# A hybrid decoder block on one core: the second MLP matrix by seven products of halves, and new first and last steps

## The chip, the cores and the metric

The kernel runs on one core of a Trainium2 chip. The metric is the device time of one execution in microseconds (us). It was run three times beside the profiled execution. The engines are named as in the profile: PE is TensorE (PEld its weight loads), DVE is VectorE, ACT is ScalarE, POOL is GpSimd, and SP is the queue that issues most of the DMA transfers.

## The reference

One decoder layer on x of 512 tokens by 1024 channels, all in float32:

```python
u = rmsnorm(x, g_norm_mix)
x = x + mixer_block(u, ...)          # mLSTM, GLA and gated DeltaNet, merged by gates, then w_out
u = rmsnorm(x, g_norm_mlp)
x = x + jnp.square(jax.nn.relu(u @ w_mlp_in)) @ w_mlp_out   # 1024 -> 4096 -> 1024
return rmsnorm(x, g_final)
```

The mixer has three branches of 4 heads of 128 channels. The root-mean-square norms divide each token by the root of its mean square. The two MLP matrices have 1024 x 4096 and 4096 x 1024 elements.

## The kernel before, in words

**Precision.** A float32 matmul is made of three matmuls of a faster type (float32r). Each operand is split into a high part (a cast to float32r) and a low part (the operand less its high part, again float32r); `mm3` (L603) issues low x high, high x low and high x high into one PSUM tile. So each weight piece costs a DMA load (`load_w`, L677, pieces of 128x1024; `load_w1`, L688, pieces of 128x512), a cast ("either": the planner picks ACT or DVE) and a subtraction on DVE. Work that is not split (transposes, attention, token sums) is plain float32 on TensorE.

**The planner.** `write_block` records every operation in a graph (`Graph.record`, L156; the profile shows all of them at L525, the line that emits). `Graph.schedule` (L243) gives an order for each engine: the split matmuls, the "mains", go to TensorE in the order of the stages in `plan` (L536); all other operations get a latest start (`due`, L275) and a list scheduler (`run`, L321) fills the engines by cost estimates, with PSUM and SBUF tiles from pools. `EVAC` (L47) says how long after its matmuls a PSUM tile should have been read, and L468 assumes DMA at 190 GB/s. The emitted order is fixed; each engine works in order.

**Pools.** 44 slots "s" of 128x512; three buffers each of "raw", "wh" and "wl" (128x1024) for weight pieces and their parts; 8 PSUM banks, four "g" for split products and four "m" for the rest.

**The first steps.** `NWARM` (L24) = 10 float32 matmuls of ones come first on TensorE. The parameters `pr` and most of the constants `cs` are loaded through POOL's queue, the rest of `cs` through ACT's. Stage "mv" (L767 to L779) multiplies the unnormalised x, in 8 k-steps, with the mv weights into four token tiles: each k-step loads an x tile and a 128x512 weight piece, scales and splits x (vh, vl), splits the weights, and issues 4 token tiles x 3 matmuls, the three of a tile together. `gen_u` (L649) squares the channel-major x tiles, adds them up on DVE, and sums over channels with `token_sums` (L638), four float32 matmuls against a column of ones; from this comes rc, 1/rms of each token.

**The MLP.** `gen_x2` (L1361) does the same sums for the second norm while it transposes x2T (channel-major) into x2 (token-major, 4 token tiles by 2 halves of 512 channels). The MLP goes by 8 groups of 512 hidden channels. `mlp_in` (L1402) makes, for each of 4 pieces of 128 hidden channels, 8 k-steps x 3 matmuls, then relu on ACT, its square as high part (`ah`, ACT), the square again on DVE (`rl`) and the low part (`al`, DVE). `mlp_out` (L1420) multiplies a group's 512 hidden channels with 512x1024 weights: 2 halves x 4 token tiles x 4 k-steps x 3 matmuls, each tile then added into x2 by one DVE instruction with the factor r2c (1/mean square of the token). The stages alternate: mi1, mo0, mi2, mo1, and so on to mi7, mo6, mo7. In the last group the tiles go half by half, the last in two pieces of 256 columns; `square_of` (L1456) sums the squares, and `finish` (L1463) takes 1/rms by a sqrt, a reciprocal and a correction, scales and stores a token tile.

Of the kernel before, what the change touches and what calls it, by code (L numbers as in the profile page):

```python
# [14 lines left out]
P = 128  # L15
# [8 lines left out]
NWARM = 10  # L24
# [22 lines left out]
EVAC = 5.0  # L47
# [62 lines left out]
class Op:  # L110
    __slots__ = ("i", "eng", "calls", "cost", "lat", "preds", "succs", "tiles", "main", "fset", "kind", "start", "fin", "lst", "npred", "ready", "new", "tag", "nbytes", "evac", "alts")


class Graph:
    def __init__(self, nc):
# [6 lines left out]
        self.gate = []  # L122
# [17 lines left out]
    def after(self, view):  # L140

        self.gate = [o for o, w, *_ in view.t.acc if w]

# [12 lines left out]
    def record(self, eng, method, a, k):  # L156
# [18 lines left out]
        self.gate = []  # L175
# [99 lines left out]
    def due(self, pin, end):  # L275
# [45 lines left out]
    def run(self, mains, caps, horizon, verbose=False):  # L321
# [19 lines left out]
        for o in ops:  # L341
            o.npred = len(o.preds)
            if any(t.cls == "m" for t in o.new):
# [44 lines left out]
        while done < total:  # L388
# [78 lines left out]
            if o.kind == "dma":  # L467
                dma_free = max(dma_free, T + 0.5) + o.nbytes / 190e3  # L468
# [67 lines left out]
def plan():  # L536

    seq = """mv mo dk0 mq1 sc mk0 dq1 dq0 mk1 mq0 dk1 gt01 dv0 gt00 dv1 gt02 lq0 gt03 gt20 up00 up02 lk0 lq1 lv lk1 up03 dz up01
    gt22 gt13 up20 gt12 gt21 up21 lr gt23 up22 up23 gt10 up10 up12 gt11 up11 up13 wo mi0""".split()
    for g in range(1, 8):  # L540
        seq += [f"mi{g}", f"mo{g - 1}"]
# [9 lines left out]
def hybrid_block(ctx, tc, xT, w_cm, w_tm, w_sc, w_up, w_out, w_mi, w_mo, w_lr, prm, cst, g_fin, out):  # L551
    nc = Graph(tc.nc)
    write_block(nc, xT, w_cm, w_tm, w_sc, w_up, w_out, w_mi, w_mo, w_lr, prm, cst, g_fin, out)
# [10 lines left out]
def write_block(nc, xT, w_cm, w_tm, w_sc, w_up, w_out, w_mi, w_mo, w_lr, prm, cst, g_fin, out):  # L564
# [58 lines left out]
    nc.gpsimd.dma_start(pr, prm)  # L623
    nc.gpsimd.dma_start(cs[:, :C_LV], cst[:, :C_LV])
# [13 lines left out]
    def token_sums(pss, sums):  # L638
        for t in range(4):
            mm(pss[:, t:t + 1], sums[:, blk(t)], ones)  # L640

    pss = mps("pss")
    rc = one("rc", [P, 4])


    for i in range(NWARM):
        mm(pss[:, P:2 * P], onem, onem)

    def gen_u():  # L649
# [8 lines left out]
        nc.vector.tensor_scalar(v, pss[:, :4], 1.0 / D, EPS, op0=ALU.mult, op1=ALU.add)  # L658
# [29 lines left out]
    def load_w1(src, name):  # L688
# [4 lines left out]
        nc.either.copy(h_, r)  # L693
# [72 lines left out]
    pmv = [gps(f"mvp{t}") for t in range(4)]  # L766
    for k in range(8):  # L767
# [9 lines left out]
        wh, wl = load_w1(w_tm[G_MV, k // 2, :, k % 2], f"mv{k}")  # L777
        for t in range(4):
            mm3(pmv[t], h_[:, blk(t)], l_[:, blk(t)], wh, wl, k == 0, k == 7)  # L779
# [11 lines left out]
    nc.scalar.dma_start(cs[:, C_LV:], cst[:, C_LV:])  # L791
# [14 lines left out]
    eall = one("em", [P, 4, 4, 2, P])  # L806
# [527 lines left out]
    def lv_evac(t, ps):  # L1334
        lv[t] = slot(f"lv{t}")
# [22 lines left out]
    pss2 = mps("pss2")  # L1358
    r2c = one("r2c", [P, 4])

    def gen_x2():  # L1361
        acc = slot("x2acc")
        for d in range(8):
            sq = tmp(f"x2sq{d}") if d else acc
            nc.scalar.activation(sq, x2T[d], AF.Square)
            if d:
                nc.vector.tensor_add(acc, acc, sq)
            if d == 7:
                token_sums(pss2, acc)
            if d % 4 == 3:  # L1370
                hf = d // 4
                for t in range(4):
# [4 lines left out]
                    nc.either.copy(x2[t][hf], ps)  # L1377
        v = small("v4", 4)
        nc.vector.tensor_scalar(v, pss2[:, :4], 1.0 / D, EPS, op0=ALU.mult, op1=ALU.add)
        nc.vector.reciprocal(r2c, v)  # L1380

# [18 lines left out]
    gf = [None, None]  # L1400

    def mlp_in(g):  # L1402
        hs_ = []
        stage[0] = f"mi{g}"
        for i in range(4):
            wh, wl = load_w(w_mi[g * 4 + i], f"mi{g}{i}")
# [11 lines left out]
        return hs_  # L1418

    def mlp_out(g, hs_):  # L1420
        last = g == NG - 1
        stage[0] = f"mo{g}"
        wts = []
        for hf in range(2):
            w_ = []
            for i in range(2):
                if last and hf:
                    w_ += [load_w1(w_mo[g, hf, i, :, kk], f"mo{g}{hf}{i}{kk}") for kk in range(2)]
                else:
                    wh, wl = load_w(w_mo[g, hf, i], f"mo{g}{hf}{i}")  # L1430
                    w_ += [(wh[:, kk], wl[:, kk]) for kk in range(2)]
            wts.append(w_)
        if last:

            for hf, t, c0, n in [(hf, t, 0, 512) for hf in range(2) for t in range(3)] + [(0, 3, 0, 512), (1, 3, 0, 256), (1, 3, 256, 256)]:
# [134 lines left out]
```

## Time and profile before

| what | value |
|---|---|
| time, median of 3 runs | 976.89 us (976.88 to 976.90) |
| the profiled execution's own time | 976.91 us |
| its span, first to last instruction | 975.1 us |
| mean granted TensorE clock | 0.996 |
| PE, DVE, ACT busy | 964.2, 580.9, 408.5 us |
| instructions | 12773 |
| DMA | 94.64 MB, mean 97 GB/s |

A profile is one execution. Busy time is the share in which an engine works on an instruction; matmuls are pipelined, so a matmul is shown as 0.39 us long though one starts every 0.23 us, and a busy TensorE may still run at half clock. What an engine waited for stands in brackets behind the row of the instruction that waited. A clock of 1.00 is 2.4 GHz and 0.50 is 1.2 GHz.

### The profile page before, as it was taken

How to read it: one execution, taken by the hardware profiler on the slowest of the kernel's cores; microseconds unless marked ns; L12 is line 12 of the kernel's file. 1: busy time of each engine (PE TensorE's matmuls, PEld its weight loads, DVE VectorE, ACT ScalarE, POOL GpSimd, SP SyncE). 2: the span in 40 equal slices, each digit the busy share in tenths (PEclk: the TensorE clock that was granted, in tenths of full speed). 3: DMA queues.
4: the chain of work that ended last, by engine and by line, in shares of the span. 5: the costliest groups of instructions: out<-in, count | busy, mean ns of one | idle time of the engine just before them, and what ended most of it. 6: DMA issues, size and time to landing. Idle time of an engine off the chain costs nothing.

```text
span 975.1 us, 12773 instructions
## 1 busy us (share of the span) xinstructions
PE 964.2 (99%) x4992; PEld 804.0 (82%) x4992; DVE 580.9 (60%) x1065; ACT 408.5 (42%) x764; POOL 5.4 (1%) x20
## 2 busy tenths in 40 slices
PE   8999999999999999999999999999999999999996
PEld 7888888888888888888888888888888888888885
DVE  6667867778525765777647665444454445544446
ACT  6454466533523664544244434442423233232313
POOL 0000000000000000000000000000000000000000
PEclk9999999999999999999999999999999999999998
DMA  7222532222411222212224222222323224322302
GB/s 269 87 87 87 170 113 95 57 87 88 123 58 66 75 98 87 88 66 76 75 89 142 96 90 94 86 98 87 108 87 109 88 84 153 128 87 87 108 22 87
DMA packets 37028, 94.64 MB, mean 97 GB/s; under 512 B 7804, under 2 KB 11900, under 8 KB 36968
## 3 DMA queue, kind: packets, MB, share of 16 engines
q1 hardware_dynamic: 36152, 92.51, 29.5%
q10 hardware_dynamic: 720, 1.08, 0.3%
q8 instruction: 39, 0.64, 0.3%
q0 software_dynamic: 96, 0.24, 0.1%
q14 instruction: 21, 0.17, 0.1%
HBM read 91.17 MB, written 2.65 MB: 96 GB/s over the span
## 4 chain that ended last, share of the span: by engine, by line
PE 98%; DVE 0%; DMA 0%; ACT 0%; issue 0%; DVEq 0%; POOLq 0%
PE mop L525 20%; PE mip L525 18%; PE upp L525 7%; PE wop L525 4%; PE mvp L525 2%; PE lrp L525 2%; PE dzp L525 2%; PE lvp L525 2%; PE ll L525 2%; PE gt22p L525 1%; PE gt13p L525 1%; PE gt20p L525 1%; PE gt12p L525 1%; PE gt21p L525 1%; PE dq0p L525 1%; PE dv0p L525 1%
## 5 line engine op out<-in xcount | busy, mean ns | idle before, releaser
L525 DVE SCALAR_TENSOR_TENSOR x<-mop,r2c,x 128x512 f32<-128x512 f32 (+1 forms) x65 | 48.1, 741 | 54.0 <-PE mop L525 53.9
L525 DVE TENSOR_TENSOR lw<-lbs 128x260 f32<-128x260 f32 (+12 forms) x52 | 21.0, 448 | 7.9 <-PE ll L525 7.8
L525 DVE SCALAR_TENSOR_TENSOR sg<-sg,upp 128x512 f32<-128x512 f32 x24 | 16.4, 685 | 15.5 <-PE upp L525 15.4
L525 ACT ACTIVATE lw<-lw 128x512 f32<-128x512 f32 x28 | 17.4, 630 | 14.1 <-DVE lw L525 13.8
L525 DVE TENSOR_TENSOR al<-rl,ah 128x512 fp32r<-128x512 f32 x32 | 22.0, 689 | 0.8
L525 DVE TENSOR_TENSOR rl<-rl 128x512 f32<-128x512 f32 x32 | 22.1, 692 | 0.0
L525 PEld LDWEIGHTS ll<-lwq,lw 128*17 128x17 f32 (+3 forms) x320 | 17.5, 131 | 4.3 <-issue 1.4
L525 ACT ACTIVATE ah<-rl 128x512 fp32r<-128x512 f32 x32 | 20.3, 634 | 1.0
L525 ACT ACTIVATE rl<-mip 128x512 f32<-128x512 f32 x32 | 18.9, 591 | 0.0
L525 ACT ACT_TABLE_LOAD x14 | 18.0, 1283 | 1.4 <-PEq L1558 1.2
L525 PE MATMUL ll<-lwq,lw 128*17 128x16 f32 (+3 forms) x320 | 17.9, 214 | 0.0
L525 DVE TENSOR_TENSOR x2T<-xr,wop 128x512 f32<-128x512 f32 x8 | 5.5, 686 | 13.3 <-PE wop L525 13.3
L525 DVE TENSOR_TENSOR lw<-lw,lks 128x260 f32<-128x260 f32 (+6 forms) x28 | 13.1, 498 | 0.0
L525 ACT COPY lAT<-ll 17x64 f32<-17x64 f32 (+3 forms) x32 | 7.2, 231 | 11.4 <-PE ll L525 11.0
L525 DVE COPY_PREDICATED lAT<-cs,ll 128x256 f32<-128x256 uint8 x16 | 9.3, 578 | 4.0 <-PE ll L525 4.0
L525 ACT ACTIVATE fsq<-x 128x512 f32<-128x512 f32 (+1 forms) x9 | 5.3, 585 | 14.1 <-DVE x L525 14.1
L525 DVE TENSOR_TENSOR me<-me,mqk 128x512 f32<-128x512 f32 (+3 forms) x16 | 7.5, 485 | 6.2 <-PE mqk L525 5.9
L525 DVE TENSOR_TENSOR sg<-sg,sg 128x512 f32<-128x512 f32 x16 | 10.8, 688 | 0.2
L525 ACT ACTIVATE cvs<-cv 128x512 f32<-128x512 f32 x12 | 7.5, 628 | 7.4 <-DVE cv L525 7.4
L525 PEld LDWEIGHTS mn<-mv,me 128*128 128x128 f32 x80 | 10.1, 191 | 0.5
L525 ACT ACTIVATE yh<-sg 128x512 fp32r<-128x512 f32 x8 | 5.1, 632 | 13.0 <-DVE sg L525 13.0
L525 PE MATMUL mqk<-mqs,mks 128*128 128x512 f32 (+3 forms) x32 | 10.4, 432 | 0.0
(1584 smaller groups left out, 3178.5 us busy)
## 6 DMA issues: line engine op xcount, KB each, us to landing
xk<-in_xT_dram SPq DMA_DIRECT2D x8, 256.0 KB, 5.6
em<-scr_rows SPq DMA_DIRECT2D x16, 128.0 KB, 4.6
xr<-in_xT_dram SPq DMA_DIRECT2D x8, 256.0 KB, 5.1
nm<-scr_rows SPq DMA_DIRECT2D x4, 256.0 KB, 3.7
out_dram<-x ACTq DMA_DIRECT2D x4, 256.0 KB, 2.1
out_dram<-x SPq DMA_DIRECT2D x4, 256.0 KB, 2.4
mo00r<-in_w_tm_dram SPq DMA_DIRECT2D x1, 512.0 KB, 6.0
mo01r<-in_w_tm_dram SPq DMA_DIRECT2D x1, 512.0 KB
```

Source lines behind the costliest of these rows:

```text
L525: getattr(getattr(nc, eng), method)(*[f(x) for x in a], **{n: f(x) for n, x in k.items()})
```

## The change

1. In groups 0 to 6 the product of a 512x512 block of hidden activations, seen as 2x2 blocks of 256, with the 512x1024 weights (2x2 blocks of 256x512) is made by Winograd's form of Strassen's algorithm: 7 products of half-size blocks in place of 8, with 4 sums of activation blocks and 4 of weight blocks ahead of them (DVE, the weight sums in place in four fixed buffers `bq`, which lie in the tile `eall` of the mixer). Products 1 and 6 accumulate over the groups in four PSUM banks; 5 and 7 in SBUF; 2, 3 and 4 are added into x2. In group 6 the shared sums are joined into x2 (`join`), and products 2 and 3 stay in PSUM, where the last group's first tiles go on.
2. `mlp_in` leaves the squares whole, in blocks by token half; the split is made later, for each product's operand.
3. The last group keeps eight products' worth of work; its tiles go token by token, its weights come in 128x512 pieces; `finish` takes the sqrt with the sum of the other pieces as its bias and fuses the multiplication by g_final.
4. The norms' sums are made token-major: x is loaded again as `x_tm` and squared with an accumulator on ACT; x2 is squared as its transposes leave PSUM. `token_sums` is gone.
5. The first steps: 9 warm-up matmuls, into the last mv tile; `pr` through ACT's queue; all of `cs` by one later load on SP's queue; the first k-step in the order high x high for four tiles, low x high for four, high x low for four; its weight cast on DVE.
6. The planner: `EVAC` 1.0 and another rule for it, 330 GB/s for DMA, "follow" (an operation that is to start after another, with no wait emitted), and stages split so that mi pieces and products alternate. lv takes mv's tiles.

```diff
-NWARM = 10
+NWARM = 9
-EVAC = 5.0
+EVAC = 1.0
...
-                l = min([l] + [pin[p] + p.cost + EVAC for p in o.preds if p in pin])
+                l = min(l, max((pin[p] + p.cost for p in o.preds if p in pin), default=1e9) + EVAC)
...
-                dma_free = max(dma_free, T + 0.5) + o.nbytes / 190e3
+                dma_free = max(dma_free, T + 0.5) + o.nbytes / 330e3
...
     for g in range(1, 8):
-        seq += [f"mi{g}", f"mo{g - 1}"]
+        seq += [x if x[0] == "p" else f"mi{g}{x[1]}" for x in "c0 p1 p5 c1 p7 p6 c2 p3 p4 c3 p2".replace("p", f"p{g - 1}").split()]
...
-    nc.gpsimd.dma_start(pr, prm)
-    nc.gpsimd.dma_start(cs[:, :C_LV], cst[:, :C_LV])
+    nc.scalar.dma_start(pr, prm)
...
     def gen_u():
-        acc = slot("xacc")
-        for k in range(8):
-            sq = tmp(f"xsq{k}") if k else acc
-            nc.scalar.activation(sq, xk[k], AF.Square)
-            if k:
-                nc.vector.tensor_add(acc, acc, sq)
-        token_sums(pss, acc)
+        ss = small("ss", 4)
+        for t in range(4):
+            b = eall.rearrange("p h c a t -> p (h c a t)")[:, blk(t, D)]
+            nc.follow(vh[4 + t // 2])
+            nc.sync.dma_start(b, x_tm[t])
+            nc.scalar.activation(b, b, AF.Square, accum_out=ss[:, t:t + 1])
...
+        wh, wl = load_w1(w_tm[G_MV, k // 2, :, k % 2], f"mv{k}", "vector" if k == 0 else None)
+        if k == 0:
+            for i, (a, b) in enumerate(((h_, wh), (l_, wh), (h_, wl))):
+                for t in range(4):
+                    with nc.group(stage[0]):
+                        nc.tensor.matmul(pmv[t], a[:, blk(t)], b, start=i == 0, stop=False)
+            continue
+        if k == 5:
+            nc.follow(x_)
+            nc.sync.dma_start(cs, cst)
...
-            a_h = slot("ah", F32R)
-            a_l = slot("al", F32R)
-            nc.scalar.activation(a_h, rl, AF.Square)
-            nc.vector.tensor_mul(rl, rl, rl)
-            nc.vector.tensor_sub(a_l, rl, a_h.bitcast(F32))
-            hs_.append((a_h, a_l))
+            for th in range(2):
+                nc.scalar.activation(a[i // 2][th][:, blk(i % 2, 256)], rl[:, blk(th, 256)], AF.Square)
...
+    def split_b(x, nm):
+        h_ = nc.tile("wh", [P, 2, 512], F32R, nm + "h")
+        l_ = nc.tile("wl", [P, 2, 512], F32R, nm + "l")
+        nc.either.copy(h_, x)
+        nc.vector.tensor_sub(l_, x, h_.bitcast(F32))
+        return h_, l_
...
+        (a11, a21), (a12, a22) = a
+        b11, b12, b21, b22 = bq
+        for x, hf, i in ((b11, 0, 0), (b12, 1, 0), (b22, 1, 1), (b21, 0, 1)):
+            nc.sync.dma_start(x, w_mo[g, hf, i])
+        tail = g == NG - 2
+        def product(n, x, y, nm):
+            stage[0] = f"p{g}{n}"
+            xh_, xl_ = split_a(x, f"a{nm}")
+            yh_, yl_ = split_b(y, f"b{g}{nm}")
+            out_ = []
+            bank = {1: p1, 6: p6, **({2: p1, 3: p6} if tail else {})}.get(n)
+            for t in range(2):
+                ps = bank[t] if bank else gps(f"pp{g}{n}{t}")
+                keepon = bank is not None
+                for k in range(2):
+                    c = slice(k * 256 + t * P, k * 256 + t * P + P)
+                    mm3(ps, xh_[:, c], xl_[:, c], yh_[:, k], yl_[:, k], k == 0 and (g == 0 or n not in (1, 6)), k == 1 and (tail and n in (1, 6) or not keepon))
+                out_.append(ps)
+            return out_
+        product(1, a11, b11, "11")
...
+        s1 = slot("S1")
+        nc.vector.tensor_add(s1, a21, a22)
+        nc.vector.tensor_sub(b11, b12, b11)
+        for t, ps in enumerate(product(5, s1, b11, "S1")):
...
+                nc.vector.tensor_add(p5[t], p5[t], ps)
+        s2 = slot("S2")
+        nc.vector.tensor_sub(s2, s1, a11)
+        nc.vector.tensor_sub(a21, a11, a21)
+        nc.vector.tensor_sub(b12, b22, b12)
+        for t, ps in enumerate(product(7, a21, b12, "S3")):
...
+        nc.vector.tensor_sub(b11, b22, b11)
+        product(6, s2, b11, "S2")
+        if tail:
+            join()
+        s4 = slot("S4")
+        nc.vector.tensor_sub(s4, a12, s2)
+        for t, ps in enumerate(product(3, s4, b22, "S4")):
...
+        nc.vector.tensor_sub(b11, b11, b21)
+        for t, ps in enumerate(product(4, a22, b11, "22")):
...
+        for t, ps in enumerate(product(2, a12, b21, "12")):
...
+        for t in range(2):
+            v = slot(f"v{t}")
+            nc.vector.tensor_add(v, us[t], p6[t])
+            add(t, 0, us[t])
+            nc.vector.tensor_add(us[t], v, p5[t])
+            add(t, 1, us[t])
+            nc.vector.tensor_add(p7[t], p7[t], v)
+            add(2 + t, 0, p7[t])
+            nc.vector.tensor_add(p5[t], p5[t], p7[t])
+            add(2 + t, 1, p5[t])
...
-        nc.scalar.activation(s, v, AF.Sqrt)
+        l = f[:, nsq[t] - 1:nsq[t]]
+        nc.scalar.activation(s, l, AF.Sqrt, bias=e)
+        nc.vector.tensor_add(v, l, e)
         nc.vector.reciprocal(y, s)
...
+        nc.vector.tensor_scalar(s, y, v, s, op0=ALU.mult, op1=ALU.add)
+        nc.vector.reciprocal(y, s)
...
+        a, b = x2[t]
+        nc.vector.scalar_tensor_tensor(b[:, 256:], b[:, 256:], y, gf[1][:, 256:], op0=ALU.mult, op1=ALU.mult)
+        nc.vector.tensor_scalar_mul(b[:, :256], b[:, :256], y)
+        nc.sync.dma_start(out[blk(t), blk(1, 512)], b)
+        nc.scalar.mul(a, a, y)
+        nc.scalar.dma_start(out[blk(t), blk(0, 512)], a)
```

## Rows read from the trace of the kernel before

**Rows 1.** The page: busy time of the engines, and the chain that ended last.
```profile
PE 964.2 (99%) x4992; PEld 804.0 (82%) x4992; DVE 580.9 (60%) x1065; ACT 408.5 (42%) x764; POOL 5.4 (1%) x20
...
PE 98%; DVE 0%; DMA 0%; ACT 0%; issue 0%; DVEq 0%; POOLq 0%
```

**Rows 2.** Stretch 700 to 960: length, busy of each engine, clock, DMA share, GB/s.
```profile
700.00:960.00 260.00, 260.00 (x1149) 215.29 (x1148) 126.83 (x156) 79.04 (x104) 0.00 (x0) 1.00 0.28 91
```

**Rows 3.** Groups by shape, DVE and ACT: busy us, mean ns of one, idle before.
```profile
L525 DVE SCALAR_TENSOR_TENSOR x<-mop,r2c,x 128x512 f32<-128x512 f32 x61 | 45.7, 749 | 52.7 <-PE mop L525 52.7
L525 DVE TENSOR_TENSOR rl<-rl 128x512 f32<-128x512 f32 x32 | 22.1, 692 | 0.0
...
L525 DVE TENSOR_TENSOR mi11l<-mi11r,mi11h 128x1024 fp32r<-128x1024 f32 x1 | 1.2, 1226 | 2.9 <-ACT mi11h L525 2.9
...
L525 DVE TENSOR_SCALAR lgw<-lge 128x512 f32<-128x512 f32 x4 | 1.7, 421 | 0.1
...
L525 ACT ACTIVATE ah<-rl 128x512 fp32r<-128x512 f32 x32 | 20.3, 634 | 1.0
L525 ACT ACTIVATE rl<-mip 128x512 f32<-128x512 f32 x32 | 18.9, 591 | 0.0
...
L525 ACT CAST mi10h<-mi10r 128x1024 fp32r<-128x1024 f32 x1 | 1.1, 1055 | 3.2 <-PE mip L525 3.2
```

**Rows 4.** Timeline of DVE in the MLP: start, length, instruction, idle before.
```profile
695.98 1.22 DVE L525 TENSOR_TENSOR mo100l<-mo100r,mo100h 128x1024 fp32r<-128x1024 f32 x1 [2.87 <-ACT mo100h L525]
697.13 0.69 DVE L525 TENSOR_TENSOR rl<-rl 128x512 f32<-128x512 f32 x1
```

**Rows 5.** Timeline of PE around the second norm's token sums.
```profile
622.39 0.95 PE L525 MATMUL pss<-ones,x2acc 128*128 128x1 f32 x8
...
623.20 0.48 PE L525 MATMUL mip<-uh,mi00l 128*128 128x512 f32 x1
...
623.52 0.39 PE L525 MATMUL mip<-ul,mi00h 128*128 128x512 f32 x1
```

**Rows 6.** Stretch 8 to 9 us, columns as in rows 2.
```profile
8.00:9.00 1.00, 1.00 (x4) 0.76 (x3) 1.00 (x2) 1.00 (x3) 0.00 (x0) 0.50 1.04 399
```

**Rows 7.** Timeline of the start, ACT and PE.
```profile
0.73 0.41 ACTq L525 DMA_DIRECT2D cs<-in_cst_dram  x1
...
1.05 3.98 PE L525 MATMUL pss<-onem 128*128 128x128 f32 x20 [1.05 <-DVE onem L525]
...
4.65 0.20 ACT L525 ACTIVATE scl<-pr 128x1 f32<-128x1 f32 x1 [2.19 <-DMA pr<-in_prm_dram]
4.76 0.70 ACT L525 ACTIVATE vh<-xk,pr 128x512 fp32r<-128x512 f32 x1
...
5.37 0.61 ACT L525 ACTIVATE xacc<-xk 128x512 f32<-128x512 f32 x1
...
5.89 0.60 ACT L525 CAST mv0h<-mv0r 128x512 fp32r<-128x512 f32 x1
...
6.54 0.51 PE L525 MATMUL mvp<-mv0h,vl 128*128 128x512 f32 x1 [1.51 <-ACT mv0h L525]
...
7.27 0.55 PE L525 MATMUL mvp<-mv0l,vh 128*128 128x512 f32 x1 [0.22 <-DVE ones L525]
...
14.24 0.39 PE L525 MATMUL mvp<-mv2h,vl 128*128 128x512 f32 x1
```

**Rows 8.** DMA issues of the start: KB each, us from issue to landing.
```profile
cs<-in_cst_dram ACTq DMA_DIRECT2D x1, 32.0 KB, 3.0
```

**Rows 9.** Timeline of the tail.
```profile
966.72 0.28 PE L525 MATMUL mop<-mo7111h,ah 128*128 128x256 f32 x1
...
968.35 0.20 ACT L525 ACTIVATE fs<-fv 128x1 f32<-128x1 f32 x1 [0.28 <-DVE fv L525]
...
968.83 0.15 DVE L525 RECIPROCAL fy<-fs 128x1 f32<-128x1 f32 x1
...
970.05 1.45 DVE L525 TENSOR_SCALAR x<-x,fy,fh 128x512 f32<-128x512 f32 x3
```

More of the change, by code (lines that the diff above doesn't have):

```diff
@@ L110 @@
 class Op:
-    __slots__ = ("i", "eng", "calls", "cost", "lat", "preds", "succs", "tiles", "main", "fset", "kind", "start", "fin", "lst", "npred", "ready", "new", "tag", "nbytes", "evac", "alts")
+    __slots__ = ("i", "eng", "calls", "cost", "lat", "preds", "succs", "tiles", "main", "fset", "kind", "start", "fin", "lst", "npred", "ready", "new", "tag", "nbytes", "evac", "alts", "soft")
 class Graph:
@@ L142, in after, with follow @@
         self.gate = [o for o, w, *_ in view.t.acc if w]
+    def follow(self, view):
+        self.soft = [o for o, w, *_ in view.t.acc if w]
     def group(self, key):
@@ L342, in run @@
             o.npred = len(o.preds)
+            for p in o.soft:
+                if p not in o.preds:
+                    waiting.setdefault(p, []).append(o)
+                    o.npred += 1
             if any(t.cls == "m" for t in o.new):
@@ L636, in write_block, with gen_u @@
     nc.vector.memset(onem, 1.0)
-    def token_sums(pss, sums):
-        for t in range(4):
[L640 to L649, printed above, removed]
-        acc = slot("xacc")
-        for k in range(8):
-            sq = tmp(f"xsq{k}") if k else acc
-            nc.scalar.activation(sq, xk[k], AF.Square)
-            if k:
-                nc.vector.tensor_add(acc, acc, sq)
-        token_sums(pss, acc)
+    eall = one("em", [P, 4, 4, 2, P])
+    rc = one("rc", [P, 4])
+    pmv = [gps(f"mvp{t}") for t in range(4)]
+    for i in range(NWARM):
+        with nc.group("warm"):
+            mm(pmv[3][:, :P], onem, onem)
+    def gen_u():
+        ss = small("ss", 4)
+        for t in range(4):
+            b = eall.rearrange("p h c a t -> p (h c a t)")[:, blk(t, D)]
+            nc.follow(vh[4 + t // 2])
+            nc.sync.dma_start(b, x_tm[t])
+            nc.scalar.activation(b, b, AF.Square, accum_out=ss[:, t:t + 1])
         v = small("v4", 4)
-        nc.vector.tensor_scalar(v, pss[:, :4], 1.0 / D, EPS, op0=ALU.mult, op1=ALU.add)
+        nc.vector.tensor_scalar(v, ss, 1.0 / D, EPS, op0=ALU.mult, op1=ALU.add)
         rsqrt(rc, v, 4)
@@ L1400, in write_block @@
     gf = [None, None]
+    bw = eall.rearrange("p h c a t -> p (h c a t)")
+    bq = [bw[:, blk(i, 1024)].rearrange("p (k n) -> p k n", k=2) for i in range(4)]
+    p1, p6 = [mps(f"P1{t}") for t in range(2)], [mps(f"P6{t}") for t in range(2)]
+    p5, p7, us = [None, None], [None, None], [None, None]
     def mlp_in(g):
-        hs_ = []
-        stage[0] = f"mi{g}"
+        a = [[slot(f"A{kh}{th}") for th in range(2)] for kh in range(2)]
         for i in range(4):
+            stage[0] = f"mi{g}{i}"
             wh, wl = load_w(w_mi[g * 4 + i], f"mi{g}{i}")
@@ new lines, in join, with add @@
+    def join():
+        def add(t, hf, v):
+            nc.vector.scalar_tensor_tensor(x2[t][hf], v, r2c[:, t:t + 1], x2[t][hf], op0=ALU.mult, op1=ALU.add)
+        for t in range(2):
+            v = slot(f"v{t}")
[7 more added lines that the diff above has]
+            add(2 + t, 1, p5[t])
@@ L1422, in mlp_out, with mlp_last @@
+    def mlp_last(a):
+        g = NG - 1
         stage[0] = f"mo{g}"
+        hs_ = [split_a(a[kh][th], f"z{kh}{th}") for kh in range(2) for th in range(2)]
         wts = []
@@ L1446, in mlp_out @@
[L1446 to L1451 removed]
+                w_ += [load_w1(w_mo[g, hf, i, :, kk], f"mo{g}{hf}{i}{kk}") for kk in range(2)]
+            wts.append(w_)
```

145 lines of the change are left out of this document (76 added, 69 removed).

## The prediction

> **What bounds the kernel now.** I read the page's totals first, then the chain that ended last, then the stretches, then the group durations. TensorE is busy 99% of the span and makes 98% of the chain [rows 1]: it is the bound, and an edit pays only if it shortens TensorE's own stream or the idle ends. The stretch from 700 to 960 us holds nothing but the MLP: 1149 matmuls in 260.00 us, 0.2263 us each, at granted clock 1.00, with VectorE busy 126.83 us (49%) and ScalarE 79.04 us (30%) [rows 2]. So there is no wait to remove there, but there is cover on the two other engines. At both ends TensorE does stand: at the start it works at half rate and waits; at the end 8 us follow its last matmul.
>
> **The sum is made** against the profiled execution's 976.91 us (span 975.1 and 1.8 around it); the runs' median is 976.89, the same to 0.02. About 0.2% (2 us) is what a measurement of this kernel can tell from no change.
>
> **1. Seven products for eight, groups 0 to 6.** Before, a group has 8 output tiles of 4 k-steps by 3 matmuls: 96. After, 7 products of 2 tiles, 2 k-steps, 3 matmuls: 84, of the same 128x512 shape. Twelve fewer in 7 groups is 84, by 0.2263 us [rows 2]: **-19.0 us**, all on the bounding engine. Group 7 keeps 96.
>
> The price is paid by VectorE. Before, a group has 8 weight subtractions of 1.226, 4 each of rl and al at 0.69 and 8 evictions of 0.749 [rows 3]: 21.3 us of a group's 192 matmuls, 43.5 us; 49%, as measured. After: 4 subtractions for the first matrix 4.9; 7 splits of an activation half (0.69) and a weight half (1.226) 13.4; 4 sums of activation halves 2.8; 4 of weight halves 4.9; 10 evictions 7.5 (products 1 and 6 stay in PSUM). That is 33.5 us in 180 matmuls, 40.7 us: 82%. Back to back the 1.22 us subtraction is followed after 1.15 us [rows 4], so nearer 76%. ScalarE: 11 casts of 1.055, 7 of about 0.63 (ah's row), 4 relu of 0.591, 8 squares of 256 columns (none is shown so far from the tail; bounds 0.32, half of ah, and 0.634; I take 0.42): 21.8 us, 54%. Neither becomes the bound on its own. The cover is thin in the last such group: joining the sums adds 16 operations (11.5) less 4 evictions (3.0), group 7's one-piece weight loads add 8 subtractions (5.5), its activation splits 4 (2.8): 50.3 us against 40.7. Some of the joining may slide into group 7's 21.7 us of matmuls, where I count 15 us of VectorE's own work; 65 us into 62.4, 95% at the back-to-back pace. What is late next is the first matmul of group 7 or the last tile. I take **+1.5 us** of waits in all; ends 0 (all covered) and 8 (a wait of about 1 us in each group and one at the join).
>
> DMA bytes of the MLP are unchanged. The weight halves now land in four fixed buffers, so their issue on SP's queue waits for the last reader, and the loads of the first matrix queue behind it; a buffer is released some 16 us (product 4's 2.7, then 5.4, 2.7 and 5.4 of matmuls) before its new content is due, against a DMA share of 0.28 [rows 2]. Nothing.
>
> **2. Token-major norms.** Both token sums leave TensorE. The second: from its first record at 622.39 to the next matmul at 623.20 is 0.81, and that matmul holds 0.32 instead of 0.23 [rows 5]: 0.90 us; the first has the same eight records: **-1.8 us**. VectorE loses 14 additions of 0.69. In their place the first norm loads x again, 2.1 MB by 4 issues on SP's queue behind the fifth and sixth x tiles; at 399 GB/s [rows 6] that is 5.3 us of transfers ahead of the later tiles. Cover: TensorE takes 2.7 us per k-step and its 0.52 MB arrive in 1.3, so the last pair, due near 26 us, lands by 20. Without that cover it costs up to 5. The second norm squares from PSUM with an accumulator, holding those banks 0.6 us longer, long before products 1 and 6 need them. Nothing.
>
> **3. The start.** The chain is [rows 7]: ScalarE waits for pr, sent through POOL's queue, until 4.65; scl; vh at 4.76; the xacc square (5.37 to 5.98); the cast mv0h to 6.49; first matmul at 6.54; then a wait until 7.27 for mv0l. After the idle 1.5 us the granted clock fell to 0.50, the 1.2 GHz level [rows 6], and the first two k-steps' 24 matmuls take until 14.24, 7.70 us where 0.2263 each would make 5.43. After: pr leaves first on ScalarE's queue, where a load issued at 0.73 landed in 3.0 us [rows 7, 8], so vh runs from about 4.1; mv0h is a VectorE copy, not shown here: 0.42 (lgw's row, one source, the nearest and the one I take) to 0.69 (rl's, two sources) [rows 3]; no square lies between. First matmul near 4.85, with the warm-up ending near 4.6 (9 of 0.4 us [rows 7]). With four matmuls of high parts first, then four with vl, then four with mv0l (0.9 us each four), VectorE's 0.75 and 0.69 for the two low parts keep ahead. Ending the second step at 10.7 in place of 14.24 is **-3.5 us**; ends -4.0 (no wait at all) and -1.2 (the clock falls again and a piece is late). Below nothing only if pr lands later than now, for which I see no reason.
>
> **4. The tail.** From the last matmul's start (966.72) to the last scaling's end (970.05 + 1.45 = 971.50): addition, sqrt at 968.35, reciprocal at 968.83, two multiplications by gf, tile 2's scalings between [rows 9]. After: the sqrt takes the sum as its bias right behind the accumulator (about 968.1), one reciprocal, a fused step, a second reciprocal (four hops of 0.15 to 0.3), then 256 columns twice on VectorE beside ScalarE's half: the last store leaves near 970.0. **-1.5 us**; ends -2.0 and +1.0 (tile 2's work still queued).
>
> **5. One answer together.** The planner's new bounds (EVAC 1.0, loads believed at 330 GB/s, soft followers, the split mi and p stages) reorder all engines. No row shows such a plan. Each change from fp32 work to the split stream costs 0.09 us on TensorE [rows 5]; twenty more or fewer are 2 us: 0, ends -2 and +2. lv's reuse of mv, the one cst load, gf's later load and the products 2 and 3 of group 6 kept in PSUM wait for things long done: nothing.
>
> Sum: -19.0 - 1.8 - 3.5 - 1.5 + 1.5 = -24.3; 976.9 - 24.3 = **952.6 us**.
>
> **The rivals.**
> B, bubbles. Products 5, 6 and 4 follow another product directly. If the three wh/wl buffers let the preparation begin only with the product ahead, their weight sum, cast and subtraction (1.226 + 1.055 + 1.226 = 3.5 us [rows 3]) stand against its 12 matmuls (2.7 us): 0.8 us, three times in 7 groups, +16.6: 969.2 us. For it: sums rewrite the weight buffers in place, and all four m banks are held through the groups. Against: a third buffer allows two stages ahead, and the order puts a 5.4 us mi stage between pairs. It decides if VectorE lags by one stage. The Trainium skill, Perfetto Trace Analysis, Optimization Strategy, reads the same gap repeating on the engine that should be saturated as too little SBUF or PSUM for the next tile; by that rule B is the case. So far the trace has no such gap [rows 2].
>
> C, slower. VectorE is in order: before each subtraction it stands until ScalarE's cast is done (2.87 us idle ahead of mo100l [rows 4]). If the casts of a group (7 by 1.055, 7 by 0.63, 4 by 1.055: 16.0 us) all fall in VectorE's way, its group takes 33.5 + 16.0 = 49.5 us, 8.8 more than TensorE's 40.7; seven times is +61.6, less the +1.5 counted: 1012.7 us. It decides once 10.7 us of a group's 16 stand so: 33.5 + 10.7 is 3.5 over 40.7, seven times that is the 24 us. Against: the emitted order interleaves independent work, so casts run a stage ahead.
>
> D, the change does not act: if the planner relaxes its order until the saved matmuls come back as waits elsewhere, 977 within 2 us.
>
> **How the numbers follow.** A, the sum, 0.74: its own range is 947.5 (no waits, -4.0, -2.0 and -2) to 958.5 (start at -1.2, a few waits more). B 0.18, spread from 958 to 972, D 0.02, C 0.06. The range 947 to 961 takes A and the half of B that is nearest: 8 in 10. Faster: A and B, 0.92; same 0.02; slower 0.06.
>
> **What would show it.** Right: 84 fewer MLP matmuls, eight fewer pss records twice; a stretch inside the MLP still at 0.226 us per matmul with TensorE 100% busy, VectorE near 76 to 82% and ScalarE near 54%; first mvp matmul before 5.2 us and clock 1.00 from 7 to 11 us; less than 7.3 us from the last matmul to the end. Wrong: TensorE idle before p5, p6 or p4 tiles, released by VectorE (B); VectorE idle behind casts while TensorE waits (C); a gap ahead of group 7's first tile; a clock of 0.50 near 9 us; loads of k-steps 5 to 7 late behind x_tm.

## The result, and the profile after the change

The changed kernel takes **953.89 us** (median of four runs, 953.58 to 954.09), the kernel before 976.88 beside it (four runs, 975.27 to 976.90): the ratio is 0.9768, 95% interval 0.9751 to 0.9785. 952.6 was forecast, 947 to 961 as the range. A second job gave 953.84 (five runs, 953.65 to 954.15) against 976.6. Three executions, one each of e1 (1969.57), e4 (3383.78) and e8 (1066.73), lie far above the other runs of the same kernel and are left out of the medians and ranges below.

The profiled execution took 953.96 us, with a span of 952.1 against 975.1. The page's totals and its chain, where [rows 1] stood before:

```profile
PE 942.1 (99%) x4890; PEld 786.2 (83%) x4890; DVE 647.3 (68%) x1146; ACT 458.5 (48%) x877; POOL 4.3 (0%) x18
...
PE 99%; DVE 0%; DVEq 0%; issue 0%
```

TensorE is still the bound: its records are 102 fewer (84 of the MLP, 16 of the two token sums, 2 of the warm-up), and VectorE has 66 us more to do. The waits view has one row for TensorE, the wait for the ones that the warm-up multiplies, which stood there before:

```profile
PE mvp L533 <- DVE onem L533: 1.1, 1, 1.1
```

Two stretches of the MLP, the first long as in [rows 2], the second one group from its product 7 to the next (columns as in [rows 2]):

```profile
700.00:940.00 240.00, 240.00 (x1061) 198.79 (x1060) 183.67 (x237) 118.03 (x187) 0.00 (x0) 1.00 0.28 92
...
700.50:741.20 40.70, 40.70 (x182) 33.69 (x181) 30.62 (x37) 20.06 (x30) 0.00 (x0) 1.00 0.32 102
```

240.00 us for 1061 matmuls is 0.2262 us each, at full clock and with TensorE never idle. VectorE is busy 76.5% of the long stretch where it was 49%, ScalarE 49% where it was 30%. Two groups by shape, of VectorE's new work and of ScalarE's squares (busy us, mean ns of one, idle before; `em` is the tile in which the weight halves now lie, `A` the block of squares):

```profile
L533 DVE TENSOR_TENSOR em<-em 128x1024 f32<-128x1024 f32 x28 | 34.1, 1219 | 0.1
L533 ACT ACTIVATE A<-rl 128x256 f32<-128x256 f32 x64 | 23.7, 411 | 3.2 <-DVE aS4l L533 2.0
```

The first row is the 28 sums of weight halves, 1.22 us each as the subtractions of [rows 3]; the squares of 256 columns take 0.411, where 0.42 was taken.

**The start.** ScalarE's, VectorE's and TensorE's timelines, which answer to [rows 7]:

```profile
3.69 0.20 ACT L533 ACTIVATE scl<-pr 128x1 f32<-128x1 f32 x1 [1.23 <-DMA pr<-in_prm_dram]
3.80 0.70 ACT L533 ACTIVATE vh<-xk,pr 128x512 fp32r<-128x512 f32 x1
```

```profile
4.50 0.43 DVE L533 CAST mv0h<-mv0r 128x512 fp32r<-128x512 f32 x1 [3.50 <-DMA mv0r<-in_w_tm_dram]
4.96 0.69 DVE L533 TENSOR_TENSOR mv0l<-mv0r,mv0h 128x512 fp32r<-128x512 f32 x1
5.57 0.75 DVE L533 SCALAR_TENSOR_TENSOR vl<-xk,pr,vh 128x512 fp32r<-128x512 f32 x1
```

```profile
5.07 1.84 PE L533 MATMUL mvp<-mv0h,vh 128*128 128x512 f32 x4
6.75 1.08 PE L533 MATMUL mvp<-mv0h,vl 128*128 128x512 f32 x4
7.67 1.08 PE L533 MATMUL mvp<-mv0l,vh 128*128 128x512 f32 x4
8.59 0.39 PE L533 MATMUL mvp<-mv1h,vl 128*128 128x512 f32 x1
...
11.31 0.39 PE L533 MATMUL mvp<-mv2h,vl 128*128 128x512 f32 x1
```

pr is there at 3.69 in place of 4.65, the first product starts at 5.07 in place of 6.54, and the third k-step at 11.31 in place of 14.24: 2.93 us won. The first four matmuls take 1.68 us (6.75 - 5.07; 0.42 each in the mean), all later ones 0.23 each. In e9, the same program run again, the first four keep nearly the full pace, and TensorE then stands until vl is done:

```profile
5.25 1.17 PE L533 MATMUL mvp<-mv0h,vh 128*128 128x512 f32 x4
6.55 1.19 PE L533 MATMUL mvp<-mv0h,vl 128*128 128x512 f32 x4
...
11.23 0.39 PE L533 MATMUL mvp<-mv2h,vl 128*128 128x512 f32 x1
```

Its third k-step starts only 0.08 us earlier. VectorE makes mv0l first and vl second (5.57 to 6.32 in the first execution), though TensorE reads vl first; so the fifth matmul could hardly have started before 6.4 there either, and at most 0.4 us of the start is the slow pace.

**The tail.** The last matmul starts at 942.92 and the span ends at 952.1. VectorE's timeline from the last reading of PSUM on, which answers to [rows 9]:

```profile
943.24 0.48 DVE L533 SCALAR_TENSOR_TENSOR x<-mop,r2c,x 128x256 f32<-128x256 f32 x1 [0.23 <-PE mop L533]
...
944.84 0.73 DVE L533 SCALAR_TENSOR_TENSOR x<-x,fy,gf 128x512 f32<-128x512 f32 x1
...
945.67 0.74 DVE L533 SCALAR_TENSOR_TENSOR x<-x,fy,gf 128x512 f32<-128x512 f32 x1
946.33 0.16 DVE L533 RECIPROCAL fy<-fs 128x1 f32<-128x1 f32 x1
946.40 1.79 DVE L533 SCALAR_TENSOR_TENSOR x<-x,fy,gf 128x512 f32<-128x512 f32 x3
948.11 0.35 DVE L533 TENSOR_SCALAR x<-x,fy 128x256 f32<-128x256 f32 x1
```

Of the three instructions in the row at 946.40 one is tile 3's own last scaling (256 columns). The other two, and those at 944.84 and 945.67, are scalings of earlier tiles, 0.73 us each, that VectorE still owes when TensorE has stopped; they stand between and behind the small steps of the last tile. From the last matmul's start to the end 9.18 us pass, where 8.38 did before (975.1 - 966.72). The old tail had a queue too: of its five scalings behind the last reading of PSUM (967.04) two are tile 3's own and three are of earlier tiles, 0.53 us each. The first of the five:

```profile
968.91 0.52 DVE L525 TENSOR_SCALAR x<-x,fy,fh 128x512 f32<-128x512 f32 x1
```

**The account** between the two profiled executions: start -2.93; 84 matmuls at 0.2263, -19.0; the two token sums, -1.8; what is left of TensorE's body, -0.07 (the last matmul starts 966.72 - 942.92 = 23.80 earlier); tail +0.80. The sum is -23.0, the difference of the spans. The groups view and the waits show that no group paid for the matmuls it lost; that the tail did, and why, is what the experiments are about.

### The profile page after: what moved, and what is told of

It reads as the page before. It is cut to its first block, busy times and chain, and to the rows that moved or that the text cites. A ratio compares the mean times of both kernels' runs of the same rounds, so it can differ in the third digit from the quotient of the medians.

```text
span 952.1 us, 12788 instructions
## 1 busy us (share of the span) xinstructions
PE 942.1 (99%) x4890; PEld 786.2 (83%) x4890; DVE 647.3 (68%) x1146; ACT 458.5 (48%) x877; POOL 4.3 (0%) x18
## 4 chain that ended last, share of the span: by engine, by line
PE 99%; DVE 0%; DVEq 0%; issue 0%
PE mip L533 18%; PE pp L533 9%; PE upp L533 7%; PE P L533 6%; PE wop L533 5%; PE mop L533 3%; PE mvp L533 3%; PE lrp L533 2%; PE dzp L533 2%; PE lvp L533 2%; PE ll L533 2%; PE gt21p L533 1%; PE gt13p L533 1%; PE gt20p L533 1%; PE gt22p L533 1%; PE gt12p L533 1%
## 5 line engine op out<-in xcount | busy, mean ns | idle before, releaser
L533 DVE TENSOR_TENSOR em<-em 128x1024 f32<-128x1024 f32 x28 | 34.1, 1219 | 0.1
L533 ACT ACTIVATE A<-rl 128x256 f32<-128x256 f32 x64 | 23.7, 411 | 3.2 <-DVE aS4l L533 2.0
L533 DVE TENSOR_TENSOR P<-P,pp 128x512 f32<-128x512 f32 x24 | 16.2, 686 | 7.6 <-PE pp L533 7.4
L533 DVE SCALAR_TENSOR_TENSOR x<-pp,r2c,x 128x512 f32<-128x512 f32 x24 | 16.9, 745 | 0.0
L533 DVE SCALAR_TENSOR_TENSOR x<-pp,r2n,x 128x512 f32<-128x512 f32 x14 | 10.5, 748 | 3.1 <-PE pp L533 3.1
L533 PE MATMUL mqk<-mqs,mks 128*128 128x512 f32 (+3 forms) x32 | 10.7, 432 | 0.0
```

Source lines behind the costliest of these rows:

```text
L533: getattr(getattr(nc, eng), method)(*[f(x) for x in a], **{n: f(x) for n, x in k.items()})
```

## The experiments

Twelve kernels. The times of one job compare best; the median of the kernel before was 976.5 in the first job (e1 to e4), 975.55 in the second (e5 to e8) and 976.6 in the third (e9 to e12). Its runs lie in two clusters, about 975.3 and 976.8, and its median moves by 1 us with the number that fall in each; so the times of the changed kernel and its variants are compared directly.

### Is it the seven products? (e1)

```diff
-        product(1, a11, b11, "11")
...
+        for hf in range(2):
+            for t in range(4):
+                ps = gps(f"mop{g}{t}{hf}")
+                for k in range(4):
...
+                    mm3(ps, ah_[:, c], al_[:, c], wts[hf][k][0], wts[hf][k][1], k == 0, k == 3)
+                nc.vector.scalar_tensor_tensor(x2[t][hf], ps, r2c[:, t:t + 1], x2[t][hf], op0=ALU.mult, op1=ALU.add)
```

> The changed kernel with only the seven products undone: groups 0 to 6 take eight products again (96 matmuls a group), each operand split once, the rest (first steps, norms, last group's tiles, planner) as changed. Theory (the matmul count is the whole gain, VectorE's extra work is hidden): 84 more matmuls at 0.2263 us, 953.9 + 19.0 = 972.9 us, within 0.7. Rival (part of the seven products' gain is taken back by waits, and the planner's new bounds gave the rest): more than 1.5 us away from 972.9, above it if waits are now in the seven-product stages.

**970.68 us** (970.38 to 970.73), ratio 0.9943 (0.9928 to 0.9959). So the seven products gain 16.8 us and not 19.0, and the rival's bound of 1.5 is passed, but not in the direction of waits. The body shows none to take away: -0.07 is all that is left of it in the account. The 2.2 us should lie at an end that the eight products leave shorter. The kept trace of e1 gives no times to compare, but the order of VectorE's instructions is fixed when the kernel is built, and the trace shows it. From the last reading of PSUM to VectorE's last instruction, no scaling of another tile lies between:

```profile
1961.19 0.48 DVE L533 SCALAR_TENSOR_TENSOR x<-mop,r2c,x 128x256 f32<-128x256 f32 x1 [1.03 <-PE mop L533]
...
1963.69 0.35 DVE L533 TENSOR_SCALAR x<-x,fy 128x256 f32<-128x256 f32 x1
```

So e1 has the tail without a queue; what that is worth at full clock, the next experiments measure.

### What the tail waits for (e2, e5, e6, e7, e9, e10)

The first attempt made the due times of the final norm of tiles 0 to 2 earlier while they are worked out, so that all that comes ahead of them is due earlier as well:

```diff
...
+            l -= o.tag
...
+                nc.hurry = 5.0 if t < 3 else 0.0
                 finish(t)
```

(`o.tag` holds the `nc.hurry` of the moment at which an operation is recorded.)

> The changed kernel with the planner told that the last norm of token tiles 0 to 2 is due 5 us earlier. Theory (after the last matmul VectorE still has five 0.73 us scalings of tiles 0 to 2 in its queue, mixed into the last tile's chain of sqrt, reciprocal, step, reciprocal): VectorE's last operation comes about 3.0 us after the last matmul's start in place of 5.5, the whole 951.5 us (2.4 less). Rival (the last stores or the chain itself set the end): within 0.5 of 953.9.

**988.03 us** (987.92 to 992.45), slower than before: ratio 1.0133 (1.0113 to 1.0153). Both expectations miss. The tail is short, 7.0 us, but the waits view of TensorE has this:

```profile
PE P L535 <- DVE aS4l L535: 11.5, 1, 11.5
PE pp L535 <- DVE aS1l L535: 7.3, 2, 4.3
PE P L535 <- DVE aS2l L535: 4.2, 4, 3.6
PE pp L535 <- DVE a22l L535: 3.1, 1, 3.1
```

The join and the additions ahead of it were moved in front of the splits for products that TensorE reads next. No instruction was added: 26 us of waits, and some slow matmuls behind them, come from VectorE's order alone. The edit was a bad test of the tail and a good one of the cover.

The next attempt lowers the due times of those operations only after all others are set:

```diff
...
+        for o in self.ops:
+            o.lst -= o.tag
...
+                nc.hurry = 8.0 if t < 3 else 0.0
                 finish(t)
```

> The changed kernel with one edit in the planner: once all due times are set, those of the operations that finish tiles 0 to 2 are made 8 us earlier (theirs alone, not those of what comes ahead of them). All arithmetic stays. In VectorE's order two scalings of 0.73 us (tile 2's) are then left behind TensorE's last matmul, where five are now, but tile 3's two multiplications by g_final (0.7 and 0.35 us) stand in the last tile's chain. Theory (queued scalings lengthen the tail): three scalings of 0.73 us go and about 0.9 us of multiplications come in, so 0.8 to 1.6 us less than 953.9, near 952.6; TensorE's stream up to the last matmul is unchanged within 0.3. Rival (the tail is the chain of stores, or of ScalarE's square and square root, and VectorE's queue is beside it): 953.9 within 0.3.

**952.79 us** (five runs, 952.58 to 953.20), 1.1 less than the changed kernel. In the third job the changed kernel itself was run again:

> The changed kernel unaltered, beside the next runs on the same chip: 953.6 to 954.1, and 9.2 us from the start of the last matmul to the end.

953.84 (953.65 to 954.15), and 9.3 us from the last matmul's start (942.84) to the end (952.1): the two sets of runs do not overlap, 953.20 against 953.58. In e5 the last matmul starts at 942.93, as in the changed kernel (942.92), and the end comes 8.07 us later. VectorE's timeline of e5:

```profile
932.71 0.16 DVE L536 RECIPROCAL fy<-fs 128x1 f32<-128x1 f32 x1 [0.40 <-ACT fs L536]
...
943.25 0.48 DVE L536 SCALAR_TENSOR_TENSOR x<-mop,r2c,x 128x256 f32<-128x256 f32 x1
...
943.77 1.41 DVE L536 SCALAR_TENSOR_TENSOR x<-x,fy,gf 128x512 f32<-128x512 f32 x2
...
946.93 0.35 DVE L536 TENSOR_SCALAR x<-x,fy 128x256 f32<-128x256 f32 x1
```

and the row of the changed kernel that answers to the first of them:

```profile
938.32 0.15 DVE L533 RECIPROCAL fy<-fs 128x1 f32<-128x1 f32 x1
```

The final norm of the first tiles starts 5.6 us earlier, two wide scalings of other tiles are left behind the last reading of PSUM in place of four (the fifth that the expectation counted starts before it), and VectorE's last instruction starts at 946.93 in place of 948.11. The end follows: 952.1 less 948.46 (the end of that instruction) is 3.6 us of storing in the one, 951.0 less 947.28 is 3.7 in the other. The tail is VectorE's queue; the rival of a tail set by the stores falls.

Two steps further along the same line, tile 3's multiplications by g_final made due earlier too, by 8 and by 12 us:

> As the run before, and tile 3's two multiplications by g_final are made due 8 us earlier as well, so that only one of them (0.35 us) is left behind the last matmul, and no wide operation stands between the two reciprocals of tile 3. Theory: 0.7 us less than the run before at most, 951.7 to 952.3, near what the eight-product variant's clean tail showed (7.1 us from the start of the last matmul to the end in place of 9.2). Rival: 953.9 within 0.3.

> As the run before with 12 us in place of 8. The order changes further ahead: some of the join's updates of tile 3 come behind the scalings of tiles 0 and 1. Theory: the tail is as in the run before or 0.3 us shorter, 951.5 to 952.3, as long as nothing of the join is late for TensorE; if a bank is freed late, a wait on TensorE of 0.5 to 5 us shows ahead of the last tiles and the gain is lost (over 952.5). Rival: 953.9 within 0.3.

**953.08** (953.04 to 953.40) and **953.4** (953.12 to 953.83): both miss, and are no better than e5. ScalarE's row in e6 says why:

```profile
944.84 0.30 ACT L536 ACTIVATE fs<-fss,fe 128x1 f32<-128x1 f32 x1 [0.67 <-DVE fe L536]
```

A scaling of another tile (943.54) and a multiplication by g_final (944.20) now stand ahead of the small sum `fe`, which is the square root's bias and came right behind the reading of PSUM in e5; so the square root starts at 944.84 where it started at 944.31 there. In e7 the last reading of PSUM itself is late, at 944.21. The last attempt moved one of tile 2's scalings to ScalarE and left VectorE one:

> The changed kernel with its last steps in another order: of tile 2's two scalings one is moved to ScalarE, behind tile 3's square root (its multiplication by g_final is made early on VectorE), and due times are set so that one scaling of 0.73 us alone is left for VectorE behind its last reading of PSUM, and tile 3's multiplications by g_final come before it. All arithmetic stays, one product is rounded in another order. Theory (VectorE's queue behind the last matmul sets the tail): 0.6 to 0.8 us less than the run with two scalings and two multiplications in the queue (which ended 8.1 us after the last matmul's start, against 9.2 of the changed kernel): about 952.1, the tail 7.4. Rival (past that point the chain through ScalarE and the stores sets it): 952.8 within 0.2, the tail 8.1.

**953.2** (953.12 to 953.52), a miss as well. The last reading of PSUM, its row here:

```profile
944.83 0.47 DVE L536 SCALAR_TENSOR_TENSOR x<-mop,r2c,x 128x256 f32<-128x256 f32 x1
```

starts 1.75 us after the last matmul (943.08), where it was 0.32 in e5. The work that no longer stands behind the reading stands in front of it. So no order tried on this line does better than e5. That none could is not shown: e11, below, ends with a shorter tail, behind a body 1.8 us longer.

### How much cover VectorE has (e8)

```diff
         nc.vector.tensor_sub(l_, x, h_.bitcast(F32))
+        for _ in range(1):
+            nc.vector.tensor_sub(l_, x, h_.bitcast(F32))
```

> The changed kernel with one more subtraction of a weight half (the same operands and result, 1.22 us) for each of the seven products of groups 0 to 6: 8.5 us of VectorE for each group. Theory (TensorE is the bound, VectorE has some 10 us of 40.7 free in a group, and an order that leaves TensorE no wait): VectorE goes to about 96% in the middle groups and over it where the sums are joined, so waits appear, 2 to 12 us: 956 to 966. Rival (bubbles at the weight sums, three buffers too few): each extra subtraction behind products 5, 6 and 4 stands in TensorE's way, 3 x 1.2 x 7 = 26 us, and with the 0.8 us that the prediction counted for each it is 980 or more.

**975.26 us** (973.62 to 977.86), ratio 0.9998 (0.9987 to 1.0010): the whole gain is gone. Both expectations miss: the theory's 956 to 966 in size, the rival's in place and, at 980 or more, in size. TensorE's two largest rows of waits; its timeline at the second of the five waits; and two of VectorE's instructions ahead of it:

```profile
PE pp L533 <- DVE aS3l L533: 12.7, 5, 2.9
PE P L533 <- DVE aS4l L533: 1.2, 1, 1.2
```

```profile
740.45 0.79 PE L533 MATMUL pp<-b2S3h,aS3l 128*128 128x512 f32 x1 [2.87 <-DVE aS3l L533]
741.04 0.63 PE L533 MATMUL pp<-b2S3l,aS3h 128*128 128x512 f32 x1
```

```profile
733.27 1.23 DVE L533 TENSOR_TENSOR b2S2l<-em,b2S2h 128x1024 fp32r<-128x1024 f32 x1 [0.17 <-ACT b2S2h L533]
...
739.71 0.69 DVE L533 TENSOR_TENSOR aS3l<-A,aS3h 128x512 fp32r<-128x512 f32 x1
```

The same wait returns in five groups, of 2.1 to 2.9 us, always at product 7, which follows a mi piece, and never at products 5, 6 or 4. VectorE has no pause of over 0.2 us there from 725 to 740: the sums and splits for products 5, 7 and 6 and a mi piece's split crowd there, and product 6's weight split (733.27) runs ahead of product 7's activation split (739.71), for which TensorE waits. The average left room (the window from 700 to 940 has VectorE busy 212.60 of 240 us, 89%); the crowded place did not. How much of a wait is the load and how much the order, which the planner makes anew, this run does not separate: product 6's two weight splits and its activation sum, 3.0 us ahead of 739.71, are as long as the wait.

A wait also costs more than its length. From a mark in the MLP's first piece (617.88, in the changed kernel 618.05) to the last matmul's start it is 347.39 us here and 324.87 there, 22.5 more, and the waits are 15.0 of it. Most of the rest, some 5 us, is the clock behind three of the waits. The windows behind the second:

```profile
740.00:741.00 1.00, 0.55 (x1) 0.50 (x2) 1.00 (x2) 0.97 (x3) 0.00 (x0) 0.62 0.00 0
741.00:742.00 1.00, 1.00 (x4) 0.76 (x3) 1.00 (x2) 0.47 (x1) 0.00 (x0) 0.50 0.00 0
```

After a pause of 2.9 us the granted clock is 0.50, the 1.2 GHz level, and the next seven steps take 0.59 and six times 0.43 us before the 0.23 returns: 1.6 us on top of the 2.87. It does not follow every wait: behind those at 785.89 and 829.32, of 2.9 and 2.1 us, the steps are back at 0.23 after one at most.

### Is it the third buffer? (e11)

```diff
-            "wh": (3, [P, 1024]), "wl": (3, [P, 1024]), ...
+            "wh": (2, [P, 1024]), "wl": (2, [P, 1024]), ...
```

> The changed kernel with two buffers for the weights' high parts and two for the low parts in place of three. The planner makes its order anew for them. Theory (TensorE runs free because preparation is a stage ahead, and the third buffer is what lets it): waits on TensorE ahead of products that follow another product, up to 1 us for each of three in seven groups, and elsewhere as much: 960 to 985. Rival (the buffers are not what the order leans on): 953.9 within 1.

**960.78 us** (960.64 to 962.05), 6.9 more, at the low end of what the theory gave, but not where it put it. TensorE's two longest waits:

```profile
PE mop L533 <- DVE mo11l L533: 3.3, 1, 3.3
PE pg L533 <- DVE bl L533: 1.5, 1, 1.5
```

Both are in the mixer, at 48.60 and 125.82 us, and with the half rate behind the first (seven steps of 0.43 us or more) the MLP starts 7.0 us late (the same mark at 625.07 for 618.05). From there to the last matmul (951.72) it takes 326.65 us for 324.87, and no product waits at all; the longest wait there is 0.5 us, ahead of a mi piece. Rival B's mechanism is not there even with two buffers, in the order that the planner makes for them.

This order happens to give a clean tail at full clock. VectorE's row behind the last reading of PSUM, and its last one:

```profile
952.26 0.48 DVE L533 SCALAR_TENSOR_TENSOR x<-mop,r2c,x 128x256 f32<-128x256 f32 x1
...
954.75 0.35 DVE L533 TENSOR_SCALAR x<-x,fy 128x256 f32<-128x256 f32 x1
```

No scaling of another tile lies between. From the last matmul's start (951.72) to the end (958.9) it is **7.18 us**: the new last steps without a queue are 1.2 shorter than the old tail with its own (8.38), and the queue adds 2.0 in the changed kernel. The 2.0 is also what e1 left open, within 0.2.

### The start (e3, e12) and the planner's bound (e4)

The first k-step's twelve matmuls in the old order, three of a token tile together:

```diff
-            for i, (a, b) in enumerate(((h_, wh), (l_, wh), (h_, wl))):
-                for t in range(4):
...
+            for t in range(4):
+                mm3(pmv[t], h_[:, blk(t)], l_[:, blk(t)], wh, wl, True, False)
```

> The changed kernel with the first k-step's twelve matmuls in the old order again (three of a tile together), so that the first waits for vl. Theory (the early start counts, and the clock): first matmul near 6.4 in place of 5.07, after an idle 1.1 us; if that idle puts the clock back to 0.50 as before the change, the third k-step starts about 3 us later, 956.5 us; if the clock holds, about 0.6 later, 954.5. Rival (the order is worth nothing, since VectorE's vl and mv0l set the pace in both): 953.9 within 0.3.

**954.58 us** (954.48 to 956.39; three of the five at 954.5, two at 956.4): three runs lie where the theory put them if the clock holds, two where it put them if the clock falls. Only one of the slower two has a trace; TensorE's timeline:

```profile
6.43 0.79 PE L533 MATMUL mvp<-mv0h,vl 128*128 128x512 f32 x1 [1.17 <-DVE vl L533]
7.02 0.63 PE L533 MATMUL mvp<-mv0l,vh 128*128 128x512 f32 x1
...
10.43 0.42 PE L533 MATMUL mvp<-mv0h,vl 128*128 128x512 f32 x1
...
13.90 0.39 PE L533 MATMUL mvp<-mv2h,vl 128*128 128x512 f32 x1
```

A wait of 1.17 us for the low part of x, then one matmul at 0.59 and eight at 0.43 us: the third k-step is at 13.90 for 11.31.

```diff
-    nc.scalar.dma_start(pr, prm)
+    nc.gpsimd.dma_start(pr, prm)
```

> The changed kernel with the parameters pr sent through the other queue (POOL's) again. Theory (the new queue is what brings the first matmul forward): pr's wait ends near 4.65 in place of 3.69, vh is done near 5.5 and the first mv matmul starts near 5.8 to 6.0 in place of 5.07; 0.6 to 1.0 us more, 954.5 to 954.9. Rival (mv0h, whose weights land at 4.5, and the half rate of the first matmuls set the start): 953.9 within 0.3.

**955.56 us** (953.78 to 956.34), four runs spread over 2.6 us: the median misses both expectations, three runs lie above the theory's 954.5 to 954.9, and the fastest, 953.78, lies at the rival's 953.9. In the profiled one, of 956.34 us:

```profile
5.83 2.08 PE L533 MATMUL mvp<-mv0h,vh 128*128 128x512 f32 x4 [0.56 <-ACT vh L533]
...
10.82 0.40 PE L533 MATMUL mvp<-mv1h,vl 128*128 128x512 f32 x1
```

The first product starts 0.76 later, as the theory had it; the second k-step starts 2.23 later (10.82 for 8.59), because twelve matmuls in place of four go at 0.42 in the mean. At full pace the twelve would end near 8.65 (an estimate: 5.83, twelve of 0.2263 us, and 0.1 for the first), where the second k-step starts at 8.59 in the changed kernel, since there the first four were slow and in e9 TensorE waited for vl. So by this estimate the queue by itself is worth next to nothing, and the run of 953.78 agrees; what the other runs lose is, in the one that was profiled, the pace behind the longer idle time.

```diff
-EVAC = 1.0
+EVAC = 5.0
```

> The changed kernel with EVAC 5.0 as before the change. Theory (the planner's bound only orders work that is hidden behind TensorE): 953.9 within 1.0, the MLP again without gaps. Rival (reading PSUM late now costs, since seven products turn over four banks twice as fast): waits of TensorE for VectorE in the MLP, 3 us or more above.

**953.76 us** (953.36 to 954.13), ratio 0.9771 (0.9757 to 0.9784): the bound alone is worth nothing that can be measured.

## Why the prediction was right, and where it was not

- **What bounds the kernel**: as read. TensorE makes 99% of the chain in place of 98%, and every term that came true is one that shortens its stream.
- **Seven products** (-19.0): TensorE lost 84 matmuls at an unchanged pace, and the body's account closes to 0.07. That this is the cause is shown by e1, with 16.8 in the end; of the 2.2 between, 2.0 is the queue in the tail (e11's measure), which e1's order does not have.
- **The waits** (+1.5, ends 0 and 8): 0, the lower end. VectorE's load was right, 30.62 of 40.70 us in a group, 75% where 76 to 82 was given; ScalarE's 20.06 us was put at 21.8. The last group, put at 95%, made no wait either: what was late there was not a matmul but the last tiles' scalings.
- **Token sums** (-1.8) and the reload of x, "nothing": both fit, by the account alone; no run undid this part by itself.
- **The start** (-3.5, ends -4.0 and -1.2): -2.93. The chain came as worked out: vh at 3.80 for 4.1, a cast of 0.43 for 0.42, a first matmul at 5.07 for 4.85. The third k-step was put at 10.7 and came at 11.31. What failed is that VectorE's two low parts "keep ahead": vl was done at 6.32, 1.25 us after the first product, where four matmuls at full pace take 0.9. By an estimate, at full pace from there the third k-step would start at 11.0 (6.4, 0.1 for the first matmul behind a wait, and twenty of 0.2263): so about 0.3 of the 0.6 us is vl, and 0.3 the slow pace of the first four. e9 has the full pace and gains only 0.08, its weights being 0.18 late. The order of the twelve is worth 0.6 us by e3's three faster runs; the queue of pr shows a gain in e12 only by way of the pace.
- **The tail** (-1.5, ends -2.0 and +1.0): this is the step that failed. The new last steps without a queue are 1.2 us shorter than the old tail (e11), near the term; but tiles 0 to 2 still had scalings in VectorE's queue, the prediction's own upper end ("tile 2's work still queued"), and that is +2.0: the sum is +0.8, and 9.18 us stand where "less than 7.3" was to show it right. The joining slid into group 7, as the first step had it, and its price was looked for in a wait of TensorE. What came late came behind TensorE's last matmul instead. That the sliding by itself made the queue is not shown: e1 has neither, but e11 has the joining as late and no queue, by another order.
- **The planner** (0, ends -2 and +2): 0 by the account; e4 says so for one of its edits. e2 shows what the term could have been: 26 us of waits from one change in due times.
- **The rivals.** B, bubbles at products 5, 6 and 4: none, with three buffers or with two. The Trainium skill, Perfetto Trace Analysis, Optimization Strategy, says that a gap that keeps repeating on the engine to be saturated can mean too little SBUF or PSUM for the next tile. Here it was the other way round: two buffers in place of three made no such gap in the MLP, and one subtraction more for each product made one of 2.1 to 2.9 us in five groups, where VectorE had a crowded stretch. C, slower, VectorE's group too long for TensorE's: not here, VectorE keeps 10 us of each group's 40.7 free and TensorE waits for nothing; but e8 shows how near it is, 8.5 us more in each group took the whole gain. D: did not happen.

The terms missed in opposite directions, the tail by +2.3 and the start by +0.6 against the waits' -1.5, so the total was off by 1.3 where single terms were off by more. That the misses partly cancel is luck. The lower end that the prediction gives its sum, 947.5, is 948.1 by its own terms (976.9 - 19.0 - 1.8 - 4.0 - 2.0 - 2.0); nothing hangs on it.

## What to carry to other kernels

Work moved off the bounding engine does not vanish: where another engine covers it in the steady state, look for it behind the bounding engine's last instruction, where nothing covers it, and put the earlier tiles' closing work ahead of it in that engine's queue, but not ahead of what the bounding engine reads next (e2). An engine busy 89% of a long stretch was full for 15 us of it (e8); the margin to ask for is that of its most crowded stretch, in the order that it has there (one instruction more for each product took all of the gain). e5 is the fastest version found here, 952.79 us, by an edit of due times alone.

## What the runs showed of the hardware

- **The clock that the windows show is not the pace at the start.** In e3's and e12's profiles every window from 5 to 12 us shows a granted clock of 1.00, while eight and nine matmuls in a row start 0.42 to 0.43 us apart. Of the kernel before, [rows 6] shows 0.50 for the same spacing. Near the start the spacing is the thing to read. By the Trainium skill, TensorE: Matmul & The Clock Gate, Part 1, 512 columns start 426.7 ns apart at the slow level; the spacing here, 0.42 to 0.43, agrees.
- **How long the slow pace lasts at the start is not settled by the program.** After the warm-up the changed kernel's first four matmuls took 0.56, 0.43, 0.43 and 0.26 us in one execution; in e9, the same program, the first took 0.31 and the next ones 0.23. e11 had a wait of 0.52 us there and then e9's pace, e12 a wait of 0.56 and twelve at 0.42 in the mean. The clusters of the kernel before (975.3 and 976.8) and of e3 (954.5 and 956.4) have the size of such a difference; that they are this was not shown, as only one execution of each is profiled.
- **A pause of TensorE of 2.9 us was followed by the 1.2 GHz level in one group and not in another** (e8, at 740.45 and at 785.89): a wait of one length has two prices, 2.9 and 4.5 us. Of the five pauses ahead of product 7, those of 2.17, 2.87 and 2.69 us were followed by seven or eight slow matmuls, those of 2.86 and 2.14 by one at most.
- A copy of 128x512 to float32r on VectorE takes 0.43 us, a weight half's sum, in place, 1.22, as the subtraction into another tile in [rows 3].
